# Last two projection units built side by side, convolution LayerNorm several tiles ahead through DRAM, and channel sums by accumulating DMA

## The chip, the cores and the metric

The kernel runs on one core of a Trainium2 chip. The metric is the time of one launch on the device in microseconds (us). The core's engines work in parallel, each in program order: TensorE (PE) multiplies, VectorE (DVE) and ScalarE (ACT) work elementwise, GpSimd (POOL) does small reductions, and SyncE (SP) issues transfers. Transfers that SP issues go by a hardware queue, those that POOL issues by a software queue; sixteen DMA engines carry both. Only transfers from the software queue add to what stands in their destination.

## The reference

One encoder layer on x of 2048 positions by 1024 channels, float32.

```python
h = rms_norm(x, norm_g)
proj = einsum("bsd,de->bse", h, w_in)
a_val, a_gate, g_conv, u, v, g_sgu = split(proj)          # 1024 columns each
c = depthwise_conv(a_val * sigmoid(a_gate), conv_w, conv_b)  # width 31
y_conv = silu(layer_norm(c, conv_ln_g, conv_ln_b)) * silu(g_conv)
y_sgu = u * (mix of layer_norm(v) inside chunks of 128 positions, per head) * silu(g_sgu)
x = x + einsum("bse,ed->bsd", concat(y_conv, y_sgu), w_out)
return rms_norm(x, final_g)
```

## The kernel before

All tiles have 128 partitions. Products take float32 operands split into a high and a low part: `split` lets ScalarE round the value to the high part and VectorE subtract it for the low part, and a product is then three passes of matmuls. The names end in `h` and `l`, or the two halves lie in one tile (`wop`, `op`, `ex`).

The work has four stages. **Group 0 and group 1** project the two halves of the positions. Each has 20 units of 256 output columns; a unit is seven products of half-size blocks in place of eight (`unit_steps`), with 12 matmuls to a product and elementwise sums between them. The operands of each product are built a few products ahead by a list of builders (`build`), seven to a unit, in the units' order. Kinds "c", "s" and "g" are the columns of the convolution, of the spatial gating and of the convolution's gate. After a unit "c" the program emits a convolution (`conv`) of 128 channels at a low priority, so that VectorE does its some 47 multiply-adds where nothing else is ready; the result goes to DRAM as `c_sp`. The tile `cx` in which it is computed comes from a pool of two places.

The **pair phase** multiplies the gating branch by its half of the output weights, two tiles of 128 positions at a time, again with seven products of 12 matmuls for each of eight pairs (`pair_steps`, L742). `pair_operands` loads `ya` and `yb` from DRAM (L718) and splits them into `yh`/`yl`, `qh`/`ql` and `ex`. The seven weight operands `wop` are made once: `wo_raw` loads the four blocks, `wo_put` splits one, `wo_plus` (L709) adds two of them in place. `early(j)` does a part of that during the last unit of group 1. Results leave by SP to `part_sp`.

The **output phase** takes 16 tiles of 128 positions with 48 matmuls each (`out_mm`, L879): the banks `po` are first filled with x plus the pair phase's part (`load_part`: x by SP, then `part_sp` accumulated on it by POOL, into a ring `pring` of four places; `seed_part`, L897, copies it to the banks), then the convolution branch is multiplied by its half of the weights (`woh`, `wol`, split from `hold`). `finish` squares the banks (L904), takes the root, scales into the ring place and stores it to `out`.

The convolution branch of a tile comes from `conv_ln`, a generator of four steps: load the eight channel blocks of 128 positions (`c_ln`, L488) and fold them to a channel sum `csum` (L494 to L496); mean by a matmul with ones, and squares; the inverse deviation; then scaling, the gate's load, silu, the product and the split into `ch` and `cl`, which stay in SBUF. `ln(...)` advances the tiles that it is given by one step each, and `ln_at` lists which steps fall into the pair phase.

A scheduler sets the order of instructions on each engine when the program is built, from these priorities and places; on the chip each engine then keeps to that order, and semaphores guard the data and the reuse of places. Pools are rings: a place comes free when the last reader of its tile is done. The pools that matter here are `wp` (8 places: `w` tiles such as `ch`, `yh`, `op`), `r4` (3 places: `ya`, `yb`, `yq`, `c_ln`), `cx` (2), and in PSUM `ps` (6 banks) and `mx` (2 banks, for the small matmuls).

Of the kernel before, what the change touches and what calls it, by code (L numbers as in the profile page):

```python
# [8 lines left out]
F32 = mybir.dt.float32  # L9
# [5 lines left out]
P = 128  # L15
S = 2048
# [15 lines left out]
def hybrid_block(ctx: ExitStack, tc: tile.TileContext, xt, x, w, wo, wst, vecs, cw, bs, fg, out):  # L32
# [38 lines left out]
    c_sp = dram.tile([NK, P, S], F32, name="c_sp")  # L71
    sgc_sp = dram.tile([NK, P, S], F32, name="sgc_sp")
# [337 lines left out]
    def unit_steps(g, ops, ring, finish):  # L410
# [9 lines left out]
        z = ptile("z")  # L420
# [24 lines left out]
    def conv(i, g):  # L445
# [33 lines left out]
        nc.gpsimd.dma_start(c_sp[i, :, 2 * m0:2 * (m0 + M)], xe.rearrange("p a n -> p (a n)")[:, :2 * M])  # L479
        tc.cur_priority = keep  # L480


    yc = {}

    def conv_ln(ti, c):
# [3 lines left out]
        t = ttile("csum")  # L489
        tt = nc.vector.tensor_tensor  # L490

        def fold(dst, src):
            if dst is not src:
                tt(dst, src[:, 0:512], src[:, 512:1024], op=add)  # L494
            tt(dst[:, 0:256], dst[:, 0:256], dst[:, 256:512], op=add)
            tt(dst[:, 0:P], dst[:, 0:P], dst[:, P:2 * P], op=add)  # L496

        fold(t, c)
# [8 lines left out]
        fold(sq[0], sq[0])  # L507
        yield
        dg = diag_cols(inv_std_cols(partition_sums(sq[0], 1), 1), 1)
        yield  # L510
# [3 lines left out]
        gt = [ttile("gate") for _ in range(2)]  # L514
        for i in range(2):
            nc.sync.dma_start(gt[i].rearrange("p (k s) -> p k s", k=4), sgc_sp[4 * i:4 * i + 4, :, sl].rearrange("k p s -> p k s"))
# [4 lines left out]
        h, l = wtile("ch"), wtile("cl")  # L521
        split(h, l, c)
        yc[ti] = (h, l)
# [56 lines left out]
    def group(g, A, vtiles):  # L580
# [69 lines left out]
        for n, (kind, i) in enumerate(units):  # L650
            steps = unit_steps(g, ops, tiles_of.setdefault(n, []), make[kind](i))
            for j in range(6):
# [21 lines left out]
                if g == 1 and n == NU - 1:  # L674
                    early(j)
# [6 lines left out]
        next(last[0], None)  # L682
        if g == 0:
            return nextA, nv

# [16 lines left out]
    def wo_put(j, q):  # L702
        wo_op[j] = t = btile([P, 2, 4, SG], F32R, f"wop{j}")
        for kp in range(2):
            split(t[:, 0, 2 * kp:2 * kp + 2, :], t[:, 1, 2 * kp:2 * kp + 2, :], raws[kp][q])

    def wo_plus(d, q):
        for kp in range(2):
            nc.vector.tensor_tensor(raws[kp][d], raws[kp][d], raws[kp][q], op=add)  # L709
# [84 lines left out]
    def early(j):  # L794
        if j == 1:
            wo_raw(0)
        if j == 2:
            wo_raw(1)
            wo_put(1, B11)
        if j == 3:  # L800
            prep(0)
            wo_plus(B11, B12)
            wo_put(5, B11)
        if j == 4:
            wo_plus(B11, B22)
            wo_put(6, B11)
            prep(0)
        if j == 5:
            wo_put(2, B21)
# [4 lines left out]
    wo_plus(B12, B22)  # L814
    wo_put(7, B12)
# [5 lines left out]
    lns = {}  # L821

    def ln(*steps):

        for ti in steps:
            if ti >= NT:
                continue
            if ti not in lns:
                c = cx.tile([P, 2, 536], F32, tag="cx", name="c_ln").rearrange("p a n -> p (a n)")[:, :1024] if ti % 4 < 2 else rtile("c_ln")
                lns[ti] = conv_ln(ti, c)  # L830
            next(lns[ti], None)

    ln_at = {(5, 3): (0,), (6, 1): (0,), (6, 3): (1,), (6, 5): (0,), (7, 0): (1, 2), (7, 1): (0,), (7, 2): (1, 3), (7, 3): (2,),
             (7, 4): (1,), (7, 5): (2,)}
    woh, wol, holds = {}, {}, {}
# [13 lines left out]
    for t in range(NT // 2):  # L849
        st = pair_steps(t, pops[t])  # L850
        for j in range(6):
# [8 lines left out]
            if t == NT // 2 - 1:  # L860
                if j == 1:
                    load_wo(0)
                if j == 2:
                    fill_wo(0)
                if j == 4:
                    load_wo(1)
                if j == 5:
                    fill_wo(1)
        last = st
    next(last, None)  # L870
    ln(3, 4)
# [9 lines left out]

    pring = btile([P, 4, 1024], F32, "pring")
    fgt = rtile("fgb")
    nc.sync.dma_start(fgt, fg.partition_broadcast(P))
    parts, pos = {}, {}

    def load_part(ti):
        if ti < NT:
            parts[ti] = pring[:, ti % 4, :]
            nc.sync.dma_start(parts[ti], x[ti * P:(ti + 1) * P, :])  # L890
            nc.gpsimd.dma_start(parts[ti], part_sp[ti], accum_op=add)
# [36 lines left out]
    for ti in range(1, NT):  # L928
        load_part(ti + 3)
# [3 lines left out]
        if ti == NT - 1:  # L933
# [54 lines left out]
```

## Time and profile before

| | before |
|---|---|
| median of 3 runs | 1404.95 us (1404.55 to 1407.33) |
| the profiled execution | 1409.1 us, its span 1407.3 us |
| mean granted TensorE clock | 0.979 of full speed |
| busy in the span: TensorE, VectorE | 1340.2 us (95%), 1190.7 us (85%) |
| busy: ScalarE, GpSimd | 588.4 us (42%), 210.2 us (15%) |
| DMA traffic | 329.15 MB, mean 234 GB/s |

The span runs from the first to the last instruction of the profiled execution. Busy shares are averages over all four stages; the rows below are from the last three of them.

### The profile page before, as it was taken

The numbers are of one execution on the slowest core, as the hardware profiler recorded it, in microseconds if no ns is written. First come the engines' busy times: TensorE is split into PE (matmuls) and PEld (weight loads), VectorE is DVE, ScalarE is ACT, GpSimd is POOL, SyncE is SP. The second block draws the span as 40 slices with busy tenths as digits, with TensorE's granted clock in tenths as the row PEclk, the third lists the DMA queues.
The fourth block names the chain that finished last, engine by engine and source line by source line (L and its number), as shares of the span: only waits on it lengthen the run. The fifth ranks groups of instructions, "written<-read, shape, count | busy, mean of one in ns | idle before, by whom it ended". The sixth has DMA issues, their size and how long they took to land. (4 is left out here: it accounts for less than half of the span.)

```text
span 1407.3 us, 17613 instructions
## 1 busy us (share of the span) xinstructions
PE 1340.2 (95%) x5948; PEld 1099.6 (78%) x5948; DVE 1190.7 (85%) x1865; ACT 588.4 (42%) x985; POOL 210.2 (15%) x394
## 2 busy tenths in 40 slices
PE   7999999999999999999999999999889996998987
PEld 5688888888888778878788888888668885876875
DVE  6985699999999899999899989999999858556753
ACT  5547534444444333443222222222524337545543
POOL 0102322323322301101001101001000001011110
PEclk9999999999999999999999999999989998998999
DMA  6228999989989874389787778787434449667761
GB/s 243 92 79 278 376 330 321 320 297 315 308 292 349 315 250 161 103 271 330 257 263 262 257 255 280 255 281 253 149 97 143 150 122 316 181 180 187 206 167 63
DMA packets 166172, 329.15 MB, mean 234 GB/s; under 512 B 14784, under 2 KB 84416, under 8 KB 166080
## 3 DMA queue, kind: packets, MB, share of 16 engines
q1 hardware_dynamic: 115456, 200.06, 43.9%
q0 software_dynamic: 33728, 119.56, 25.1%
q10 hardware_dynamic: 16896, 8.39, 2.1%
q8 instruction: 47, 0.77, 0.2%
q14 instruction: 45, 0.37, 0.1%
HBM read 191.12 MB, written 136.84 MB: 233 GB/s over the span
## 5 line engine op out<-in xcount | busy, mean ns | idle before, releaser
L469 DVE SCALAR_TENSOR_TENSOR ca<-cx,cwt,ca 128x505 f32<-128x505 f32 (+1 forms) x240 | 180.0, 750 | 0.0
L471 DVE SCALAR_TENSOR_TENSOR cb<-cx,cwt,cb 128x504 f32<-128x504 f32 (+1 forms) x224 | 167.9, 750 | 6.5 <-ACT cb L465 2.8
L477 DVE SCALAR_TENSOR_TENSOR cb<-cq,cws,cb 128x504 f32<-128x504 f32 (+1 forms) x224 | 167.2, 746 | 0.3
L347 PE MATMUL x<-s,op 128*128 128x512 f32 x624 | 153.1, 393 | 1.6 <-ACT s L129 1.4
L347 PEld LDWEIGHTS x<-s,op 128*128 128x128 f32 x624 | 117.7, 189 | 26.7 <-ACT s L129 1.7
L198 PE MATMUL v<-vh,a 128*128 128x512 f32 x448 | 121.0, 393 | 3.8 <-ACT a L129 3.4
L198 PEld LDWEIGHTS v<-vh,a 128*128 128x128 f32 x448 | 84.2, 189 | 23.3 <-ACT a L129 4.2
L347 PE MATMUL z<-s,op 128*128 128x512 f32 x336 | 82.0, 391 | 0.6 <-DVE s L130 0.5
L347 PE MATMUL x<-s,ex 128*128 128x512 f32 x336 | 81.4, 390 | 0.0
L879 PE MATMUL po<-woh,ch 128*128 128x512 f32 x256 | 70.3, 415 | 10.4 <-ACT ch L129 10.4
L347 PE MATMUL x<-a,op 128*128 128x512 f32 x312 | 79.2, 391 | 0.0
L347 PE MATMUL v<-a,op 128*128 128x512 f32 x312 | 75.4, 390 | 2.9 <-DVE t L434 2.9
L347 PE MATMUL y<-a,op 128*128 128x512 f32 x312 | 76.1, 391 | 0.2 <-DMA op<-op_sp 0.2
L347 PE MATMUL v<-s,op 128*128 128x512 f32 x312 | 75.3, 390 | 0.0
L347 PEld LDWEIGHTS z<-s,op 128*128 128x128 f32 x336 | 62.7, 188 | 14.2 <-DVE s L130 0.9
L347 PEld LDWEIGHTS x<-s,ex 128*128 128x128 f32 x336 | 62.9, 188 | 13.0
L130 DVE TENSOR_TENSOR op<-w,op 128x512 fp32r<-128x512 f32 x92 | 62.0, 688 | 10.8 <-ACT op L129 10.8
L347 PEld LDWEIGHTS v<-a,op 128*128 128x128 f32 x312 | 58.3, 188 | 16.3 <-DVE t L434 4.2
L198 PE MATMUL v<-vl,a 128*128 128x512 f32 x224 | 68.5, 394 | 0.9 <-DVE vl L130 0.9
L320 POOL DMA_DIRECT2D op_sp<-op x92 | 49.2, 535 | 133.9 <-DVE op L130 127.9
L129 ACT ACTIVATE op<-w 128x512 fp32r<-128x512 f32 x92 | 54.9, 625 | 33.6 <-DVE w L323 23.5
L347 PEld LDWEIGHTS y<-a,op 128*128 128x128 f32 x312 | 58.4, 188 | 13.1 <-DMA op<-op_sp 0.6
(198 smaller groups left out, 2721.0 us busy)
## 6 DMA issues: line engine op xcount, KB each, us to landing
op_sp<-op POOLq DMA_DIRECT2D x92, 512.0 KB, 6.1
op<-op_sp SPq DMA_DIRECT2D x92, 512.0 KB, 4.8
op_sp<-ex POOLq DMA_DIRECT2D x48, 512.0 KB, 5.8
ex<-op_sp SPq DMA_DIRECT2D x48, 512.0 KB, 5.0
w<-in_w_dram SPq DMA_DIRECT2D x40, 512.0 KB, 7.1
vraw<-in_w_dram SPq DMA_DIRECT2D x32, 256.0 KB, 4.8
mix_sp<-mixt ACTq DMA_DIRECT2D x32, 256.0 KB, 6.4
glu_sp<-sig POOLq DMA_DIRECT2D x64, 128.0 KB, 4.6
```

Of the source, the lines that this page charges most:

```text
L129: nc.scalar.activation(hi, src, AF.Copy)
L130: nc.vector.tensor_tensor(lo, src, hi.bitcast(F32), op=sub)
L198: nc.tensor.matmul(pss[c], A[b, k // 4][:, apart, k % 4, c * P:(c + 1) * P], tiles[k // 2][wpart][:, :, k % 2, :], start=k == 0 and p == 0 ...
L320: nc.gpsimd.dma_start(op_sp[n * 7 + j], t)
L347: nc.tensor.matmul(acc, tv[:, wpart, kk, :], a[:, apart, kk, :], start=start and p == 0 and kk == 0, stop=p == 2 and kk == 3, skip_group_c ...
L469: stt(a, e[:, j:j + M + 1], cwt[:, i, 2 * j:2 * j + 1], a, mul, add)
L471: stt(b, o[:, j:j + M], cwt[:, i, 2 * j + 1:2 * j + 2], b, mul, add)
L477: stt(b, q[:, j:j + M], cws[:, i, j:j + 1], b, mul, add)
L879: nc.tensor.matmul(po[h], lw[:, b * 4 + k, :], rh[:, k, h * SG:(h + 1) * SG], start=False, stop=stop and p == 2 and k == 3, skip_group_che ...
```

## The change

Three things change together, and the places of buffers with them.

The last two units of group 1 (both of kind "s") no longer run one behind the other: their steps alternate, product by product, and their 14 builders alternate too. The bank `z` of both comes from the pool `mx`. `early(j)` runs after each such pair of steps, and the weight operands of the pair phase are split in finer pieces inside it, with those of `wop7` moved in from behind the group.

The convolution's LayerNorm no longer keeps `ch` and `cl` from the LayerNorm to the product: its result is stored to DRAM (`yc_sp`) by POOL, and `load_y` brings it back by SP and splits it two tiles ahead of its use. LayerNorm itself runs three to five tiles ahead; its tiles `c_ln` come from `cx` for the first five and then from a new ring `cring` of four places. The ring `pring` has three places for parts, since its fourth holds the final norm's weights. The gates are loaded one step earlier. The parts and the `yc` of tiles 0 and 1 are loaded during pair 7.

The channel sum is no longer folded by VectorE: each convolution's result is also sent to DRAM `cs_sp`, the first as a store and the other seven of a group as accumulating transfers, and LayerNorm loads 128 columns of it.

```diff
-        nc.gpsimd.dma_start(c_sp[i, :, 2 * m0:2 * (m0 + M)], xe.rearrange("p a n -> p (a n)")[:, :2 * M])
+        flat = xe.rearrange("p a n -> p (a n)")[:, :2 * M]
+        nc.gpsimd.dma_start(c_sp[i, :, 2 * m0:2 * (m0 + M)], flat)
+        if i == 0:
+            nc.gpsimd.dma_start(cs_sp[:, 2 * m0:2 * (m0 + M)], flat)
+        else:
+            nc.gpsimd.dma_start(cs_sp[:, 2 * m0:2 * (m0 + M)], flat, accum_op=add)
         tc.cur_priority = keep
...
     def conv_ln(ti, c):
         sl = slice(ti * P, (ti + 1) * P)
         c3 = c.rearrange("p (k s) -> p k s", k=NK)
         nc.sync.dma_start(c3, c_sp[:, :, sl].rearrange("k p s -> p k s"))
         t = ttile("csum")
+        nc.sync.dma_start(t[:, 0:P], cs_sp[:, sl])
...
-        fold(t, c)
         yield
...
         dg = diag_cols(inv_std_cols(partition_sums(sq[0], 1), 1), 1)
+        gt = [ttile("gate") for _ in range(2)]
+        for i in range(2):
+            nc.sync.dma_start(gt[i].rearrange("p (k s) -> p k s", k=4), sgc_sp[4 * i:4 * i + 4, :, sl].rearrange("k p s -> p k s"))
         yield
...
         for k in range(NK):
             nc.scalar.activation(c3[:, k, :], c3[:, k, :], AF.Silu, bias=cln_b[:, k:k + 1], scale=cln_g[:, k:k + 1])
         for i in range(2):
             tt(c[:, i * SG:(i + 1) * SG], c[:, i * SG:(i + 1) * SG], gt[i], op=mul)
-        h, l = wtile("ch"), wtile("cl")
-        split(h, l, c)
-        yc[ti] = (h, l)
+        nc.gpsimd.dma_start(yc_sp[ti], c)
...
+        if g == 1:
+            tail = builders[-14:]
+            builders[-14:] = [tail[i * 7 + j] for j in range(7) for i in range(2)]
...
-                if g == 1 and n == NU - 1:
-                    early(j)
...
+        both = [unit_steps(g, ops, tiles_of.setdefault(n, []), make[units[n][0]](units[n][1]), xtile) for n in (NU - 2, NU - 1)]
+        for j in range(6):
+            next(both[0])
+            build()
+            if j == 0:
+                next(last[0], None)
+            next(both[1])
+            build()
+            early(j)
+        for steps in both:
+            next(steps, None)
...
     def early(j):
+        if j == 0:
+            wo_raw(0)
         if j == 1:
-            wo_raw(0)
+            wo_put(1, B11, (0,))
         if j == 2:
             wo_raw(1)
-            wo_put(1, B11)
+            wo_plus(B11, B12, (0,))
+            wo_put(5, B11, (0,))
+            wo_put(1, B11, (1,))
         if j == 3:
+            wo_plus(B11, B12, (1,))
+            wo_put(5, B11, (1,))
             prep(0)
-            wo_plus(B11, B12)
-            wo_put(5, B11)
-        if j == 4:
             wo_plus(B11, B22)
             wo_put(6, B11)
+        if j == 4:
             prep(0)
+            wo_put(2, B21)
         if j == 5:
-            wo_put(2, B21)
+            wo_plus(B12, B22)
+            wo_put(7, B12)
     A1, nv = group(0, A, vtiles)
     group(1, A1, nv)
-    wo_plus(B12, B22)
-    wo_put(7, B12)
     wo_put(3, B22)
     wo_plus(B11, B21)
     wo_put(4, B11)
...
@@ -826,13 +844,35 @@
             if ti >= NT:
                 continue
             if ti not in lns:
-                c = cx.tile([P, 2, 536], F32, tag="cx", name="c_ln").rearrange("p a n -> p (a n)")[:, :1024] if ti % 4 < 2 else rtile("c_ln")
+                c = cx.tile([P, 2, 536], F32, tag="cx", name="c_ln").rearrange("p a n -> p (a n)")[:, :1024] if ti < 5 else cring[0][:, ti % 4, :]
                 lns[ti] = conv_ln(ti, c)
             next(lns[ti], None)
-    ln_at = {(5, 3): (0,), (6, 1): (0,), (6, 3): (1,), (6, 5): (0,), (7, 0): (1, 2), (7, 1): (0,), (7, 2): (1, 3), (7, 3): (2,),
-             (7, 4): (1,), (7, 5): (2,)}
-    woh, wol, holds = {}, {}, {}
+    ln_at = {}
+    for i in range(4):
+        for n in (0, 2, 5, 7)[:2 if i == 3 else 4]:
+            ln_at.setdefault(divmod(27 + 5 * i + n, 6), []).append(i)
+    yc = {}
+    def load_y(ti):
+        if ti < NT:
+            r = rtile("yc")
+            nc.sync.dma_start(r, yc_sp[ti])
+            h, l = wtile("ch"), wtile("cl")
+            split(h, l, r)
+            yc[ti] = (h, l)
+    woh, wol = {}, {}
+    parts, pos, pring = {}, {}, []
+    def load_part(ti):
+        if ti < NT:
+            parts[ti] = rtile("part") if ti < 2 else pring[0][:, ti % 3, :]
+            nc.sync.dma_start(parts[ti], x[ti * P:(ti + 1) * P, :])
+            nc.gpsimd.dma_start(parts[ti], part_sp[ti], accum_op=add)
...
             ln(*ln_at.get((t, j), ()))
             if t == NT // 2 - 1:
                 if j == 1:
+                    load_part(0)
+                if j == 2:
                     load_wo(0)
-                if j == 2:
                     fill_wo(0)
+                if j == 3:
+                    load_y(0)
                 if j == 4:
+                    load_part(1)
                     load_wo(1)
+                    load_y(1)
                 if j == 5:
                     fill_wo(1)
         last = st
     next(last, None)
-    ln(3, 4)
+    ln(4)
...
-    for ti in range(3):
-        load_part(ti)
+    pring.append(btile([P, 4, 1024], F32, "pring"))
+    cring.append(btile([P, 4, 1024], F32, "cring"))
+    fgt = pring[0][:, 3, :]
+    nc.sync.dma_start(fgt, fg.partition_broadcast(P))
+    load_part(2)
     seed_part(0)
     seed_part(1)
-    out_mm(pos[0], yc[0], 0, (0, 1), False)
-    ln(2, 3)
-    load_part(3)
-    out_mm(pos[1], yc[1], 0, (0, 1), False)
-    ln(4, 5)
-    out_mm(pos[0], yc[0], 1, (0, 1), True)
-    seed_part(2)
-    finish(0)
-    for ti in range(1, NT):
-        load_part(ti + 3)
+    for ti in range(NT):
+        if ti:
+            load_part(ti + 2)
+        load_y(ti + 2)
         po = pos[ti]
         if ti > 1:
             seed_part(ti + 1)
-        if ti == NT - 1:
+        if ti == 0:
+            out_mm(po, yc[0], 0, (0, 1), False)
+            ln(3, 4)
+            out_mm(pos[1], yc[1], 0, (0, 1), False)
+            out_mm(po, yc[0], 1, (0, 1), True)
+            ln(3, 5)
+            seed_part(2)
+        elif ti < NT - 1:
+            if ti > 1:
+                out_mm(po, yc[ti], 0, (0, 1), False)
+            ln(ti + 3, ti + 4)
+            out_mm(po, yc[ti], 1, (0, 1), True)
+            ln(ti + 3, ti + 5)
+        else:
             for h in range(2):
                 out_mm(po, yc[ti], 0, (h,), False)
                 out_mm(po, yc[ti], 1, (h,), True)
-        else:
-            if ti > 1:
-                out_mm(po, yc[ti], 0, (0, 1), False)
-            ln(ti + 2, ti + 3)
-            out_mm(po, yc[ti], 1, (0, 1), True)
-            ln(ti + 4, ti + 5)
         finish(ti)
```

How the order of instructions moves is shown at three places. The first is VectorE in front of pair 3's first low part, the last row of each excerpt (`ca`, `cb`, `cq` and `cx` are convolutions, `ex` and `ql` operands of pair 2, `oz` and `c` results of a pair). Before:

```order
L777 TENSOR_TENSOR oz_8370<-oz_8370,ox 128x512
L469 SCALAR_TENSOR_TENSOR ca<-cx,cwt,ca 128x521
L477 SCALAR_TENSOR_TENSOR cb<-cq,cws,cb 128x520
L130 TENSOR_TENSOR ex_8213<-ya,ex_8213 128x512
L469 SCALAR_TENSOR_TENSOR ca<-cx,cwt,ca 128x521
L478 SCALAR_TENSOR_TENSOR cx<-cq,cws,cb 128x520
L130 TENSOR_TENSOR ex_8213<-yb,ex_8213 128x1024
L469 SCALAR_TENSOR_TENSOR ca<-cx,cwt,ca 128x521
L130 TENSOR_TENSOR yl<-ya,yh 128x1024
```

The changed kernel:

```order
L744 SCALAR_TENSOR_TENSOR ya<-yq,ya 128x512
L132 TENSOR_TENSOR ql<-yq,qh 128x1024
L473 SCALAR_TENSOR_TENSOR cb<-cx,cwt,cb 128x520
L790 TENSOR_TENSOR oz_8388<-oz_8388,ox 128x512
L132 TENSOR_TENSOR ex_8231<-ya,ex_8231 128x512
L473 SCALAR_TENSOR_TENSOR cb<-cx,cwt,cb 128x520 x4
L132 TENSOR_TENSOR ex_8231<-yb,ex_8231 128x1024
L473 SCALAR_TENSOR_TENSOR cb<-cx,cwt,cb 128x520
L132 TENSOR_TENSOR yl<-ya,yh 128x1024
```

Before, the end of the last convolution but one (`cx<-cq`) stands four rows ahead of `yl`. Now it is fifteen rows ahead, outside the excerpt, and operations of the last convolution take its place. Counted from the start of the program up to this `yl`, there are 9 more convolution operations than before.

The second place is SP, from the load of `ya` for pair 2 or 3 on (`co`, `c` and `oz` are stores of a pair's results). Before, from pair 3's `ya`:

```order
L718 DMA ya<-y_sp 128x8x128
L747 DMA part_sp<-oz_8370 128x512
L747 DMA part_sp<-co 128x512
L718 DMA yb<-y_sp 128x8x128
L488 DMA c_ln<-c_sp 128x8x128
L747 DMA part_sp<-co 128x512
L718 DMA ya<-y_sp 128x8x128
```

The changed kernel, from pair 2's `ya`:

```order
L731 DMA ya<-y_sp 128x8x128
L731 DMA yb<-y_sp 128x8x128
L760 DMA part_sp<-co 128x512
L760 DMA part_sp<-c_8448 128x512
L493 DMA c_ln<-c_sp 128x8x128
L731 DMA ya<-y_sp 128x8x128
L760 DMA part_sp<-oz_8388 128x512
L731 DMA yb<-y_sp 128x8x128
```

The first load of LayerNorm (`c_ln<-c_sp`) stood behind both loads of pair 3; now it stands ahead of them.

The third is TensorE at the end of pair 7 (`ov` and `ox` are its last products, `pc`, `pm` and `rb_c` the small LayerNorm matmuls, `po` the output tiles). Before:

```order
L742 MATMUL ox<-wop_8201,ex_8213 128x512 x12
L512 MATMUL rb_c<-dg,ones 128x128
L742 MATMUL ov<-wop_8208,ex_8213 128x512 x12
L124 MATMUL pc<-ones,csq 128x1
L501 MATMUL pm<-csum,ones 128x128
L512 MATMUL rb_c<-dg,ones 128x128
L124 MATMUL pc<-ones,csq 128x1
L501 MATMUL pm<-csum,ones 128x128
L879 MATMUL po<-woh_9183,ch 128x512 x4
L879 MATMUL po<-woh_9183,cl 128x512 x4
```

The changed kernel:

```order
L126 MATMUL pc<-ones,csq 128x1
L755 MATMUL oy<-wop_8121,yh 128x512 x3
L755 MATMUL ov<-wop_8170,ex_8231 128x512 x4
L755 MATMUL ox<-wop_8219,ex_8231 128x512 x12
L924 MATMUL po<-woh_9285,ch 128x512 x7
L755 MATMUL ov<-wop_8170,ex_8231 128x512 x8
L924 MATMUL po<-woh_9285,ch 128x512
L924 MATMUL po<-woh_9285,cl 128x512 x8
L514 MATMUL rb_c<-dg,ones 128x128
```

The small matmuls of three tiles' LayerNorm stood between the last product and the first output tile. Now one stands between, and the output tile's matmuls begin ahead of the last 8 of pair 7. In each later period of the output phase SP has two loads more, the channel sum and `yc`, and POOL a store to `yc_sp`.

## Rows read from the trace of the kernel before

**Rows 1.** Windows by stage: PE, PEld, DVE, ACT, POOL busy, clock, DMA share, GB/s.

```profile
985.00:1070.40 85.40, 73.75 (x298) 57.06 (x297) 82.58 (x105) 36.52 (x47) 2.69 (x5) 0.92 0.39 130
1070.40:1165.00 94.60, 94.60 (x423) 78.36 (x422) 70.80 (x100) 35.79 (x50) 1.11 (x2) 1.00 0.46 144
1165.00:1191.70 26.70, 14.98 (x61) 11.68 (x59) 24.00 (x37) 20.68 (x40) 4.80 (x7) 0.81 1.01 326
1191.70:1377.00 185.30, 170.82 (x745) 139.03 (x744) 111.82 (x209) 96.15 (x218) 26.93 (x38) 0.94 0.70 183
1377.00:1400.10 23.10, 22.07 (x96) 17.94 (x96) 7.93 (x13) 7.62 (x19) 1.08 (x2) 1.00 0.11 46
```

**Rows 2.** The critical chain at the first product of pair 3.

```profile
1070.44 2.72 PE ox L742 x12
```

**Rows 3.** Waits of TensorE, 985 to 1056: total, times, longest.

```profile
PE ox L742 <- DVE wop L130: 5.2, 1, 5.2
```

**Rows 4.** The critical chain through one round of the part ring.

```profile
1357.22 4.86 DMA out_dram<-pring
1362.10 3.53 DMA pring<-in_x_dram
1365.67 0.46 issue
1366.15 5.42 DMA pring<-part_sp
...
1371.65 1.12 ACT po L897 x2
```

**Rows 5.** Waits in the output phase, 1191.7 to 1400.

```profile
ACT po L897 <- DMA pring<-part_sp: 35.4, 7, 7.4
...
PE po L879 <- ACT ch L129: 10.4, 5, 3.8
```

**Rows 6.** Timeline of VectorE around the end of the fourteenth convolution.

```profile
1060.54 0.76 DVE L469 SCALAR_TENSOR_TENSOR ca<-cx,cwt,ca 128x521 f32<-128x521 f32 x1
1061.21 0.75 DVE L477 SCALAR_TENSOR_TENSOR cb<-cq,cws,cb 128x520 f32<-128x520 f32 x1
...
1063.16 0.75 DVE L478 SCALAR_TENSOR_TENSOR cx<-cq,cws,cb 128x520 f32<-128x520 f32 x1
```

**Rows 7.** Timeline of SP's DMA issues in front of pair 3.

```profile
1060.05 0.37 SPq L718 DMA_DIRECT2D ya<-y_sp  x1
...
1070.24 0.37 SPq L488 DMA_DIRECT2D c_ln<-c_sp  x1
```

**Rows 8.** DMA issues, 1165 to 1191.7: count, size, median us to landing.

```profile
pring<-in_x_dram SPq DMA_DIRECT2D x4, 512.0 KB, 4.9
pring<-part_sp POOLq DMA_DIRECT2D x4, 512.0 KB, 11.8
```

**Rows 9.** DMA queues of the output phase: packets, MB, share of 16 engines.

```profile
q1 hardware_dynamic: 30132, 27.28, 42.5%
q0 software_dynamic: 2101, 7.62, 21.0%
```

**Rows 10.** DMA queues over the whole span, from the page.

```profile
q0 software_dynamic: 33728, 119.56, 25.1%
```

**Rows 11.** Windows around single transfers, and one of the burst (as rows 1).

```profile
1382.00:1385.00 3.00, 3.00 (x15) 2.49 (x14) 1.82 (x2) 1.06 (x1) 0.00 (x0) 1.00 0.43 175
1111.00:1114.50 3.50, 3.50 (x18) 2.88 (x17) 3.36 (x6) 0.19 (x1) 0.00 (x0) 1.00 0.53 150
...
1186.00:1198.00 12.00, 7.70 (x26) 6.04 (x26) 6.28 (x12) 7.61 (x16) 1.42 (x2) 0.62 1.08 240
```

**Rows 12.** Instructions on the tile csum: durations min/median/max in ns.

```profile
L494 DVE TENSOR_TENSOR csum<-c_ln x16: 683/685/693, 1126.2 to 1351.9; 128x512 f32<-128x512 f32 x16
```

**Rows 13.** Timeline of ScalarE: first square of one tile's finish.

```profile
1272.28 0.58 ACT L904 ACTIVATE pring<-po 128x512 f32<-128x512 f32 x1
```

**Rows 14.** Timeline of SP: the output store of that tile.

```profile
1278.37 0.62 SPq L914 DMA_DIRECT2D out_dram<-pring  x1
```

More of the change, by code (lines that the diff above doesn't have):

```diff
@@ L71, in hybrid_block @@
     c_sp = dram.tile([NK, P, S], F32, name="c_sp")
+    cs_sp = dram.tile([P, S], F32, name="cs_sp")
+    yc_sp = dram.tile([NT, P, D], F32, name="yc_sp")
     sgc_sp = dram.tile([NK, P, S], F32, name="sgc_sp")
@@ L408, in finish_g, with unit_steps @@
         return gate, value, False
-    def unit_steps(g, ops, ring, finish):
+    def unit_steps(g, ops, ring, finish, zbank):
         gate, value, odd_first = finish
@@ L419, in unit_steps @@
         yield
-        z = ptile("z")
+        z = zbank("z")
         product(z, s1, ring.pop(0), True)
@@ L478, in conv @@
         stt(res[:, :, 1], q[:, 15:], cws[:, i, 15:16], b, mul, add)
-        nc.gpsimd.dma_start(c_sp[i, :, 2 * m0:2 * (m0 + M)], xe.rearrange("p a n -> p (a n)")[:, :2 * M])
+        flat = xe.rearrange("p a n -> p (a n)")[:, :2 * M]
[4 more added lines that the diff above has]
+            nc.gpsimd.dma_start(cs_sp[:, 2 * m0:2 * (m0 + M)], flat, accum_op=add)
         tc.cur_priority = keep
-    yc = {}
     def conv_ln(ti, c):
@@ L489, in conv_ln @@
         t = ttile("csum")
+        nc.sync.dma_start(t[:, 0:P], cs_sp[:, sl])
         tt = nc.vector.tensor_tensor
[L492 to L496, printed above, removed]
-        fold(t, c)
         yield
@@ L506, in conv_ln @@
         tt(sq[0], sq[0], sq[1], op=add)
-        fold(sq[0], sq[0])
+        tt(sq[0][:, 0:256], sq[0][:, 0:256], sq[0][:, 256:512], op=add)
+        tt(sq[0][:, 0:P], sq[0][:, 0:P], sq[0][:, P:2 * P], op=add)
         yield
         dg = diag_cols(inv_std_cols(partition_sums(sq[0], 1), 1), 1)
+        gt = [ttile("gate") for _ in range(2)]
+        for i in range(2):
+            nc.sync.dma_start(gt[i].rearrange("p (k s) -> p k s", k=4), sgc_sp[4 * i:4 * i + 4, :, sl].rearrange("k p s -> p k s"))
         yield
@@ L513, in conv_ln @@
         tt(c3, c3, rb[:, None, :P].broadcast_to([P, NK, P]), op=mul)
-        gt = [ttile("gate") for _ in range(2)]
-        for i in range(2):
-            nc.sync.dma_start(gt[i].rearrange("p (k s) -> p k s", k=4), sgc_sp[4 * i:4 * i + 4, :, sl].rearrange("k p s -> p k s"))
         for k in range(NK):
@@ L650, in group @@
         for n, (kind, i) in enumerate(units):
-            steps = unit_steps(g, ops, tiles_of.setdefault(n, []), make[kind](i))
+            if g == 1 and n == NU - 2:
+                break
+            steps = unit_steps(g, ops, tiles_of.setdefault(n, []), make[kind](i), ptile)
             for j in range(6):
@@ L681, in group @@
             last = (steps, kind, i)
-        next(last[0], None)
         if g == 0:
+            next(last[0], None)
             return nextA, nv
+        both = [unit_steps(g, ops, tiles_of.setdefault(n, []), make[units[n][0]](units[n][1]), xtile) for n in (NU - 2, NU - 1)]
[3 more added lines that the diff above has]
+            if j == 0:
+                next(last[0], None)
+            next(both[1])
[3 more added lines that the diff above has]
+            next(steps, None)
     wo_op, raws = {}, [[], []]
@@ L700, in wo_raw, with wo_put, wo_plus @@
             raws[kp].append(r)
-    def wo_put(j, q):
-        wo_op[j] = t = btile([P, 2, 4, SG], F32R, f"wop{j}")
-        for kp in range(2):
+    def wo_put(j, q, kps=(0, 1)):
+        if j not in wo_op:
+            wo_op[j] = btile([P, 2, 4, SG], F32R, f"wop{j}")
+        t = wo_op[j]
+        for kp in kps:
             split(t[:, 0, 2 * kp:2 * kp + 2, :], t[:, 1, 2 * kp:2 * kp + 2, :], raws[kp][q])
-    def wo_plus(d, q):
-        for kp in range(2):
+    def wo_plus(d, q, kps=(0, 1)):
+        for kp in kps:
             nc.vector.tensor_tensor(raws[kp][d], raws[kp][d], raws[kp][q], op=add)
@@ L819, in hybrid_block @@
     ex2.append(btile([P, 4, 1024], F32R, "ex2"))
-    lns = {}
+    lns, cring = {}, []
     def ln(*steps):
@@ L880, in out_mm @@
                                      stop=stop and p == 2 and k == 3, skip_group_check=True)
[L882 to L891, printed above, removed]
     def seed_part(ti):
```

## The prediction

> **What bounds the kernel now.** The page gives TensorE the largest busy share, but an average says little, so I read the stages first [rows 1]. At full clock 12 matmuls of a pair take 2.72 us [rows 2], 0.2267 us each; a stage's time less its matmuls at that price is what TensorE loses there.
>
> - 1070.4 to 1165 (pairs 3 to 7): busy throughout at clock 1.00. Nothing is to be won.
> - 985 to 1070.4 (end of the last unit, pairs 0 to 2): 298 matmuls are worth 67.6 us of 85.4, so 17.8 are lost. VectorE is busy 82.58 of 85.4, and TensorE's longest single wait is for VectorE's half of a `wop` split [rows 3]. VectorE is the bound.
> - 1165 to 1191.7 (end of pair 7, start of the output phase): 61 matmuls are worth 13.8 of 26.7, so 12.9 are lost. The DMA share is 1.01: the loads for the output phase come in one burst.
> - 1191.7 to 1400.1: 16 tiles of 48 matmuls are 768 x 0.2267 = 174.1 of 208.4. The 73 small LayerNorm matmuls I put at 6 us (0.08 each, between nothing and 0.2267); about 28 are lost. The chain there [rows 4] runs from an output store through the `x` load into the same ring place, the accumulating load of `part_sp` and its copy into the banks. The waits agree [rows 5]: 35.4 us of ScalarE behind `part_sp`, 10.4 of TensorE behind the split `ch` of LayerNorm's result.
> - From 1400.1 to the span's 1407.3: 7.2 us for the last tile's norm and store.
>
> **Part 1: the last two units and the wop splits.** This stage is VectorE's, so I count VectorE's instructions. The splits move earlier; none is removed. What matters is what the order puts ahead of the pairs' own operands: up to the fourth `yl<-ya` (pair 3) the changed kernel has 9 more convolution operations and nothing less. Such an operation takes 0.75 us alone, but starts stand 0.67 apart [rows 6], so 9 x 0.67 = 6.0 us more work lie in front of pair 3; up to its `ql` it is 6 operations, 4.0 us. I take +5, the middle of the two. Bounds: -17.8, if two units side by side give VectorE enough slack that it is not waited for; +12, if the late `ya` below adds to the 6.
>
> The new wait here is on SP. Pair 3's `ya` was issued at 1060.05, ten microseconds before the first `c_ln` load [rows 7]; now that `c_ln` load stands ahead of it. It takes the `cx` place of the last convolution but one. That one's last operation started at 1063.16 [rows 6]; the new order has it a dozen rows earlier against `yl`, but with more work ahead, so I leave it there. The place now comes free only behind a store to `c_sp` and an accumulation into `cs_sp`. An accumulating load lands in 5.42 [rows 4], so SP gets past it at about 1068; `ya` follows some 4 us later, and pair 3's first product, at 1070.44 before [rows 2], comes at about 1074. Queued behind are the stores of pair 2's results, which nothing waits for before the output phase. It overlaps the 5 us, so I don't add it.
>
> **Part 2: the gap.** `part` and `yc` of tiles 0 and 1 and the `hold` loads are issued inside pair 7, and LayerNorm of tiles 0 to 3 starts earlier. In the new order tile 0's first matmuls stand ahead of pair 7's last 8, and most of the small LayerNorm matmuls that stood between are gone from there. So most of the 12.9 goes: I take -13. Bounds: 0, if these loads still land as late as in the burst (11.8 for a part [rows 8]); -15, with the early matmuls of tile 0.
>
> **Part 3: the output phase.** TensorE's floor is 28 below. Against it stands DMA time, priced as share times time:
> - By queue in this phase [rows 9], over 208.4 us: the hardware queue's 42.5% for 27.28 MB is 3.25 us per MB; the software queue's 21.0% for 7.62 MB is 5.75, so one accumulating part of 0.524 MB costs all sixteen engines 3.0 us. Over the whole kernel, with plain stores for the most part, that queue's 25.1% of 1407.3 is 2.95 per MB [rows 10]: 1.55 for a `yc` store.
> - By short stretches [rows 11]: an `out` store alone is 3.0 x 0.43 = 1.3; a `ya` load alone, in rows of 512 bytes like `c_ln` and the gates, is 3.5 x 0.53 = 1.9.
>
> A period of the changed kernel is out 1.3, x 1.3, part 3.0, gates 1.9, `c_ln` 1.9, `yc` store 1.55 and load 1.3, and a channel sum of 64 KB at 3.25 per MB, 0.2: 12.5 us. TensorE's 48 matmuls are 10.9, with the small ones 11.2. Before, the DMA sum was 9.4. So the DMA engines become the bound as long as LayerNorm runs.
>
> From 1165 on before needs 26.7 x 1.01 + 185.3 x 0.70 + 23.1 x 0.11 = 159 us of DMA [rows 1]. The change adds 14 stores x 1.55, 16 loads x 1.3 and 13 sums x 0.2, 45: 204. About 5 go into pair 7, at a share of 0.46 until 1165; some 43 fall behind tile 9, where LayerNorm is done (three periods of 10.7, one of 7, one of 4). The 156 between, at a share of 1.03 (1.01 and 1.08 where it is saturated [rows 1, 11]), take 151 us from 1170 (1165 + 5): to 1321. TensorE is then about at tile 9's end, 1319; six tiles at 11.2 are 67, the tail 7.2: span 1393. Parts 1 and 2 alone give 1399, so the phase itself yields 6 of its 28.
>
> **A rule against the trace.** In 1186 to 1198 the share was 1.08 at 240 GB/s [rows 11]. The Trainium skill ("DMA: Bandwidth & Descriptors", section "Where 436 GB/s comes from") puts the ceiling at 435 GB/s through 16 ports. By it a period's 3.7 MB would be an estimated 8.6 us, and DMA would not bind. The trace does not agree for this mix, where accumulations cost 5.75 us per MB and rows of 512 bytes half more than whole ones. What the rule would give is the first rival.
>
> **Costed at nothing.** The three folds of the channel sums go (the first takes 0.685 us, 16 times [rows 12]). In the output phase VectorE is busy 111.82 of 185.3, so they save only latency, and LayerNorm now runs three to five tiles ahead. The 16 transfers into `cs_sp`, 0.52 MB or 3.0 us each, stand beside the convolutions, the last ones where the pairs leave the DMA share at 0.39 to 0.46 [rows 1]; each waits for the one before it and holds its `cx` place longer. If a convolution stands still for one: up to +6.
>
> **Sum.** 1407.3 + 5 - 13 - 6 = 1393. The profiled execution took 1409.1 us, the median of the runs is 1404.95; -14 from that is **1391**.
>
> **Rivals.**
> - DMA keeps up and TensorE binds the output phase. For it: the share of 0.70 before. Against it: the prices above. From 1165 the pair's last 13.8 and tile 0's 10.9 lead to 1190; 15 x 11.2 and 7.2 give 1365, with the +5 of part 1 1370: 1363 to 1368 us. Chance 0.14; the skill's rule comes out here.
> - Part 1 gains: side by side, the units fill VectorE's waits and the 17.8 come back in place of +5. 1391 - 23 = 1368. Against it: VectorE is 97% busy there, with more in front. Chance 0.09.
> - No effect: LayerNorm's lead is not what held the phase; the DMA engines reach 0.95 only, as the transfers that wait for one another allow. The 156 take 164 us, the span is 1406, 1404 us. Chance 0.06.
> - Slower: the part ring has three places, not four, so a load can start only a tile later. One round is the finish (6.1 from the first square to the store [rows 13, 14]), out 4.86, x 3.53, issue 0.5, part 5.42, copies 1.1 [rows 4], matmuls 11.2: 32.7 us for three tiles, 10.9 a tile, which leaves no slack at all. In the burst a part takes 11.8, 2.2 times as long, and x 4.9, 1.4 times [rows 8]; with out longer by the one or the other it is 42.4 or 46.2, 14.1 or 15.4 a tile, and at 14.7 the span is 1190 + 15 x 14.7 + 7.2 = 1418, about 1415 us. From 14.2 a tile it is slower than before. Chance 0.18, because a saturated DMA is what I forecast.
>
> The forecast has 0.53, with 1380 to 1402 as its own range. The range for 8 in 10 reaches to the near ends of the fast rivals and of the ring: 1368 to 1413. No change is within 0.2%, 2.8 us, about what runs of this kernel can tell: 1402.1 to 1407.8. Faster: 0.48 of the forecast and both fast rivals, 0.71. Same: no effect and the forecast's upper edge, 0.09. Slower: the ring and the worst of part 1, 0.20.
>
> **What would show it.** Right: pair 3's first product three to five microseconds late with VectorE above 95% ahead of it; no gap before the first `po`; a DMA share of at least 0.95 and 12 to 12.5 us a tile over the first ten tiles, about 11 after. Wrong: 11 us a tile from the start (DMA was no bound); the loss before pair 3 gone (part 1 gains); ScalarE's copies waiting on `part_sp` at 14 us a tile (the ring).

## Result: 3.2% slower, and the profile after

The median is 1451.36 us (4 runs, 1448.82 to 1457.9) against 1406.14 for before (4 runs): ratio 1.0324, 95% interval 1.0283 to 1.0365. It lies outside the forecast range and on its other side. The profiled execution took 1451.84 us with a span of 1450.1.

The windows of the changed kernel (columns as in [rows 1], and three stretches ahead of them):

```profile
0.00:520.00 520.00, 498.18 (x2220) 409.55 (x2220) 446.89 (x731) 248.98 (x404) 127.80 (x242) 0.99 0.82 279
520.00:700.00 180.00, 167.72 (x773) 139.34 (x774) 169.55 (x268) 64.85 (x96) 18.71 (x32) 0.95 0.66 214
700.00:985.00 285.00, 282.42 (x1239) 233.40 (x1238) 264.12 (x389) 71.42 (x104) 35.64 (x73) 0.99 0.81 271
985.00:1076.00 91.00, 80.98 (x334) 64.03 (x333) 86.41 (x110) 36.91 (x49) 6.85 (x13) 0.94 0.50 168
1076.00:1200.80 124.80, 120.34 (x521) 98.36 (x520) 86.78 (x118) 52.31 (x81) 6.03 (x8) 0.97 0.61 181
1200.80:1443.00 242.20, 202.94 (x867) 164.30 (x866) 119.90 (x201) 113.75 (x252) 37.66 (x57) 0.92 0.77 231
```

The last three rows answer to those of [rows 1]: the first to its first, the second to its next two, the third to its last two. Before, up to 985 us:

```profile
0.00:985.00 985.00, 964.00 (x4333) 795.57 (x4334) 891.89 (x1401) 391.09 (x613) 173.02 (x340) 0.99 0.78 264
```

Counting how many matmuls are done by a given time, at 0.2267 us each, places the loss. The changed kernel has done 2220 + 773 + 1239 = 4232 by 985 us, before 4333: **22.9 us are lost in the two groups**, of which the prediction said nothing. By 1040 us only some 9 of them are left, by 1080 it is 21 again, at 1200 it is 13.4: most of the gap ahead of the output phase is gone, as forecast. (The counts take the small LayerNorm matmuls at the same price; with the matmuls of 512 columns alone it is 11.6 at 1200.) Then the output phase, from the first `po` at 1200.83 to the end of the matmuls at 1443, takes 242 us where before needed 208: **the second loss**, 29 us by the counts (13.4 behind at 1200, 42.8 at the end). Its DMA share is 0.77, far from the 1.03 that the sum stood on. Only its first 39 us, up to 1240, are at such a share:

```profile
1200.80:1220.00 19.20, 17.53 (x80) 14.21 (x79) 13.92 (x18) 11.76 (x23) 4.65 (x6) 1.00 1.07 353
1220.00:1240.00 20.00, 11.04 (x49) 8.77 (x47) 4.52 (x8) 6.78 (x16) 1.10 (x2) 0.84 1.07 298
```

From 1240 to 1443 the share is 0.71.

In the groups, TensorE's waits from 470 to 700 us (engine, what it waited for, total, times, longest) are these; the same stretch of before has none above 1.8 us:

```profile
PE z L349 <- ACT s L131: 4.6, 1, 4.6
PE x L349 <- ACT s L131: 4.2, 1, 4.2
PE v L349 <- DVE t L436: 3.0, 1, 3.0
PE v L200 <- ACT vh L131: 2.9, 1, 2.9
```

Waiting is not the whole of the 22.9 us. Up to 985 us TensorE is busy for 948.3 us against 964.0, so 15.7 are idle time; the other 7 are matmuls that took longer, at a lower granted clock. The clearest stretch holds the two longest waits:

```profile
620.00:640.00 20.00, 11.12 (x36) 8.59 (x35) 19.96 (x38) 8.62 (x11) 2.97 (x3) 0.74 0.56 200
```

At full clock the 36 matmuls are 8.2 us; here, with a granted clock of 0.74 on average, TensorE is busy with them for 11.1.

The first wait of the list is for the high part of a block sum `s`, which ScalarE makes when VectorE has its `r`. VectorE's timeline ahead of that `r`, the last row (`ca` and `cb` are operations of a convolution):

```profile
621.86 0.72 DVE L471 SCALAR_TENSOR_TENSOR ca<-cx,cwt,ca 128x505 f32<-128x505 f32 x1
...
622.76 0.69 DVE L479 SCALAR_TENSOR_TENSOR cb<-cq,cws,cb 128x504 f32<-128x504 f32 x1
623.37 0.68 DVE L172 TENSOR_TENSOR r<-a 128x512 f32<-128x512 f32 x1
...
624.09 0.69 DVE L471 SCALAR_TENSOR_TENSOR ca<-cx,cwt,ca 128x505 f32<-128x505 f32 x1
624.70 0.73 DVE L479 SCALAR_TENSOR_TENSOR cb<-cq,cws,cb 128x504 f32<-128x504 f32 x1
625.36 0.68 DVE L173 TENSOR_TENSOR r<-r,r 128x512 f32<-128x512 f32 x1
```

VectorE is not idle; four of these rows are convolution operations, on the path of a waiting TensorE. Before has such rows at this place too, so these rows alone do not explain the wait; the experiments take up what does.

In the output phase the waits that answer to [rows 5] are:

```profile
ACT po L931 <- DMA pring<-part_sp: 40.2, 9, 10.6
...
ACT ch L131 <- DMA yc<-yc_sp: 33.5, 9, 6.7
...
PE po L924 <- ACT ch L131: 25.9, 6, 6.5
...
PE pm L499 <- DMA csum<-cs_sp: 7.3, 2, 6.1
```

`po` waits for `ch` 2.5 times as long as before, and `ch` waits for its load from `yc_sp`. The chain at one such place:

```profile
1264.48 5.24 DMA yc_sp<-c_ln
...
1269.74 5.88 DMA yc<-yc_sp
...
1275.63 0.03 ACT ch L131
```

```profile
1276.74 3.78 PE L924 MATMUL po<-woh,ch 128*128 128x512 f32 x8 [4.41 <-ACT ch L131]
```

LayerNorm's result goes out in 5.2 us and comes back in 5.9, and only then is split; TensorE (the last row, from its timeline) has waited 4.4 us for it. SP shows the second mechanism:

```profile
1210.05 15.51 SPq L493 DMA_DIRECT2D cring<-c_sp  x4
1225.65 3.09 SPq L760 DMA_DIRECT2D part_sp<-c  x1
```

Four LayerNorm loads for the new ring hold SP for 15.5 us, since all four places come with one tile. The stores of pair 7, the first output and the channel sum that TensorE's next `pm` needs stand behind them.

### The profile page after: what moved, and what is told of

It reads as the page before. It is cut to its first block, busy times and chain, and to the rows that moved or that the text cites. A ratio compares the mean times of both kernels' runs of the same rounds, so it can differ in the third digit from the quotient of the medians.

```text
span 1450.1 us, 17718 instructions
## 1 busy us (share of the span) xinstructions
PE 1353.3 (93%) x5948; PEld 1109.3 (76%) x5948; DVE 1175.4 (81%) x1817; ACT 588.9 (41%) x985; POOL 233.2 (16%) x426
## 5 line engine op out<-in xcount | busy, mean ns | idle before, releaser
L924 PE MATMUL po<-woh,ch 128*128 128x512 f32 x256 | 75.8, 436 | 28.9 <-ACT ch L131 25.9
L349 PE MATMUL z<-s,op 128*128 128x512 f32 x348 | 86.2, 395 | 5.9 <-ACT s L131 4.6
L924 PEld LDWEIGHTS po<-woh,ch 128*128 128x128 f32 x256 | 51.8, 210 | 42.5 <-ACT ch L131 28.1
L349 PEld LDWEIGHTS z<-s,op 128*128 128x128 f32 x348 | 65.9, 191 | 20.2 <-ACT s L131 5.1
L349 PE MATMUL y<-a,op 128*128 128x512 f32 x324 | 79.3, 391 | 0.0
L349 PE MATMUL x<-a,op 128*128 128x512 f32 x300 | 76.1, 391 | 0.0
L349 PEld LDWEIGHTS x<-s,ex 128*128 128x128 f32 x348 | 65.1, 188 | 13.4
L420 ACT ACTIVATE y<-x 128x512 f32<-128x512 f32 x40 | 23.3, 581 | 122.1 <-PE x L349 122.1
```

The costliest lines, as they stand in the source:

```text
L349: nc.tensor.matmul(acc, tv[:, wpart, kk, :], a[:, apart, kk, :], start=start and p == 0 and kk == 0, stop=p == 2 and kk == 3, skip_group_c ...
L420: nc.scalar.activation(y, x0, AF.Copy)
L924: nc.tensor.matmul(po[h], lw[:, b * 4 + k, :], rh[:, k, h * SG:(h + 1) * SG], start=False, stop=stop and p == 2 and k == 3, skip_group_che ...
```

## Experiments

Times are medians; ratios are to the runs of before on the same chip, whose median lay between 1407.5 and 1408.4 us. "Ahead" and "behind" are against before, counted in matmuls as above, each from one profiled execution.

### Each part alone

**cs_only**: before, with the third part alone.

```diff
+        if i == 0:
+            nc.gpsimd.dma_start(cs_sp[:, 2 * m0:2 * (m0 + M)], flat)
+        else:
+            nc.gpsimd.dma_start(cs_sp[:, 2 * m0:2 * (m0 + M)], flat, accum_op=add)
...
+        nc.sync.dma_start(t[:, 0:P], cs_sp[:, sl])
...
-        fold(t, c)
```

> Before plus only the third part: the channel sums by accumulating transfers, no folds. Theory (the changed kernel lost 20 to 23 us in the two groups because the transfers into the channel sums hold the convolution's places longer and shift the convolution's operations on VectorE in front of the group's own): it shows that loss alone, 20 to 26 us slower than before, 1425 to 1432 us, with TensorE some 85 to 105 matmuls behind at 900 us. Rival (the group loss comes from another part of the change): within 3 us of before.

Measured 1435.46 us, 1.0195 (1.0163 to 1.0227), 27 us slower, a little more than the theory's 20 to 26, and 26.8 us behind at 980 us. The loss in the groups belongs to the channel sums.

**after_nocs**: the changed kernel without it.

```diff
-            nc.gpsimd.dma_start(cs_sp[:, 2 * m0:2 * (m0 + M)], flat, accum_op=add)
...
-        nc.sync.dma_start(t[:, 0:P], cs_sp[:, sl])
+        tt(t, c[:, 0:512], c[:, 512:1024], op=add)
+        tt(t[:, 0:256], t[:, 0:256], t[:, 256:512], op=add)
+        tt(t[:, 0:P], t[:, 0:P], t[:, P:2 * P], op=add)
```

> The changed kernel with the third part undone (three folds on VectorE, no channel sums in memory). Theory (as for cs_only): the loss in the groups goes, and with it the waits for the sum's load in the output phase: 20 to 30 us faster than the changed kernel, 1421 to 1431 us; what is left above before is the output phase's. Rival: within 3 us of the changed kernel's 1451.

Measured 1422.4 us, 1.0096 (1.0071 to 1.0121): 29 us faster than the changed kernel, as the theory has it, and still slower than before.

**side_only**: before, with the first part alone (`early` with its pieces, too).

```diff
+        both = [unit_steps(g, ops, tiles_of.setdefault(n, []), make[units[n][0]](units[n][1]), xtile) for n in (NU - 2, NU - 1)]
+        for j in range(6):
+            next(both[0])
+            build()
...
+            next(both[1])
+            build()
+            early(j)
```

> Before plus only the first part: last two units side by side, weight operands split earlier. Theory of the prediction (VectorE binds this stretch and has more in front): 0 to 5 us slower than before, 1405 to 1411 us. Rival, suggested by the changed kernel's trace (TensorE regains 14 us from 985 to 1040 and gives part of it back by 1060): 5 to 14 us faster, 1391 to 1400 us.

Measured 1398.24 us, 0.9928 (0.9899 to 0.9956), 10 us faster: the rival, not the prediction. One window of before, then the same of side_only:

```profile
985.00:1060.00 75.00, 63.35 (x252) 48.46 (x251) 72.89 (x92) 31.32 (x40) 2.16 (x4) 0.91 0.35 119
```

```profile
985.00:1060.00 75.00, 70.07 (x306) 56.72 (x304) 73.74 (x94) 34.75 (x45) 2.17 (x4) 1.00 0.41 134
```

Before did 252 matmuls there with VectorE busy 72.89 us. Here VectorE is as busy, and TensorE does 306: 12.2 us gained. Some 7 of them are idle time that is gone (TensorE busy 70.07 us in place of 63.35); the rest is the granted clock, 1.00 in place of 0.91. Its only waits up to 1075 us are four, of 1.9 us at most.

**ln_only**: before, with the second part alone, folds kept.

```diff
-        h, l = wtile("ch"), wtile("cl")
-        split(h, l, c)
-        yc[ti] = (h, l)
+        nc.gpsimd.dma_start(yc_sp[ti], c)
...
+            parts[ti] = rtile("part") if ti < 2 else pring[0][:, ti % 3, :]
```

> Before plus only the second part: LayerNorm ahead through memory, three places for parts, early loads in pair 7, folds kept. Theory (the round trip store, load, split and the burst of four LayerNorm loads on SP cost more than the lead gains): the output phase is 15 to 25 us longer, the gap before it 5 to 10 us shorter, so 5 to 20 us slower than before, 1410 to 1426 us. Rival (the output phase of the changed kernel suffers only from the channel sums' loads): faster than before by 5 to 15 us.

Measured 1423.7 us, 1.0113 (1.0091 to 1.0135). It is 12.2 us ahead at 1200 us, so the gap's gain is real. It is 13.1 behind at 1400 us: the output phase costs 25. The first piece is one wait at its start, in TensorE's row and in SP's:

```profile
1211.74 0.76 PE L495 MATMUL pm<-csum,ones 128*128 128x128 f32 x2 [9.09 <-DVE csum L492]
```

```profile
1187.48 11.74 SPq L487 DMA_DIRECT2D cring<-c_sp  x3
...
1203.14 1.44 SPq L487 DMA_DIRECT2D c_ln<-c_sp  x1
```

Three loads into the ring hold SP for 11.7 us; tile 4's `c_ln`, which `pm` needs, comes behind them.

Alone the parts come to -10, +27 and +15, together 32; the changed kernel is 45 slower. The first two together give +14 (after_nocs), not +5: of the 11.8 us that the units win by 1060, only 2.5 are left at 1200 (14.7 ahead against ln_only's 12.2). What opens the output phase starts no earlier for them.

### What in the channel sums costs it

**cs_plain**: a second plain store, nothing added, folds kept.

```diff
+        nc.gpsimd.dma_start(c2_sp[i, :, 2 * m0:2 * (m0 + M)], xe.rearrange("p a n -> p (a n)")[:, :2 * M])
```

> Before plus a second plain store of each convolution's result to a place of its own in memory; the folds stay, nothing is accumulated. In the groups its order of instructions is that of cs_only, row for row on VectorE. Theory (order and the longer hold of the convolution's place cost the time, not the adding): 15 to 27 us slower than before, 1421 to 1435 us. Rival (the accumulating transfers' own price and their chain): within 5 us of before.

Measured 1430.09 us, 1.0153 (1.0106 to 1.02). At 980 us it is 10.4 behind. Its order on TensorE, ScalarE, VectorE and SP is that of cs_only all through the groups, up to 16 convolution operations ahead of before's on VectorE; so by these counts some 16 of cs_only's 26.8 us come from the adding, and 10.4 from one more transfer with the order that goes with it. The total was as the theory forecast; the split was not. The size of the split is rough: cs_only's profiled execution is the longest of its four, cs_plain's the shortest, and the medians are only 5.4 us apart. That the adding costs time in the groups rests on all four profiles with it (cs_only, cs_dram, best_cs and the changed kernel), which stand 23 to 29 us behind at 985. DMA issues of cs_only over the span, then of cs_plain (its two stores of a result are one row):

```profile
c_sp<-cx POOLq DMA_DIRECT2D x8, 504.0 KB, 4.8
cs_sp<-cx POOLq DMA_DIRECT2D x8, 504.0 KB, 8.2
```

```profile
c_sp<-cx POOLq DMA_DIRECT2D x16, 504.0 KB, 4.9
```

An accumulating transfer takes 3 us longer to land. From 735 to 780 us of cs_only the waits behind it are, on SP's queue and then on the engines:

```profile
SPq L459 <- DMA cs_sp<-cx: 7.4, 1, 7.4
```

```profile
DVE m L388 <- DMA m<-mix_sp: 7.3, 2, 6.7
...
PE v L348 <- DVE t L435: 3.9, 1, 3.9
```

SP waits with the next convolution's load, so what is queued behind it is late; VectorE waits for its `m`, and TensorE, for 3.9 us, for VectorE's `t`. In cs_plain SP's wait there is 3.0 us, and VectorE has none for `m`.

**cs_dram**: the adding transfers read the first copy.

```diff
-            nc.gpsimd.dma_start(cs_sp[:, 2 * m0:2 * (m0 + M)], flat, accum_op=add)
+            nc.gpsimd.dma_start(cs_sp[:, 2 * m0:2 * (m0 + M)], c_sp[i, :, 2 * m0:2 * (m0 + M)], accum_op=add)
```

> As cs_only, but the accumulating transfers read the result from its first copy in memory, so the convolution's place comes free with the first store as in before. Order in the groups as in cs_only. Theory 1 (the order costs the time): 20 to 27 us slower than before. Theory 2 (the longer hold on the chip costs it): within 6 us of before.

Measured 1425.92 us, 1.0119 (1.0077 to 1.0161): 18 us slower, between the two theories, and 28.6 behind at 980 us. Freeing the place early does not help in the groups, so theory 2 falls. Theory 1 isn't shown by it either: the adding is still there and lands in 8.7 to 9.2 us, and from the middle of group 0 its order departs from that of cs_only in places.

**cs_tiny8**: 4 KB in place of 0.5 MB.

```diff
+        nc.gpsimd.dma_start(c2_sp[i, :, 2 * m0:2 * m0 + 8], xe.rearrange("p a n -> p (a n)")[:, :8])
```

> Before plus one more transfer per convolution from its place, of 8 columns only (4 KB), folds kept: no bytes to speak of, but the order on VectorE shifts by up to 7 convolution operations (16 in cs_plain). Theory (the order costs the time): slower than before by 4 to 14 us, 1412 to 1422 us. Rival (bytes on the DMA engines cost it): within 3 us of before.

Measured 1416.56 us, 1.0074 (1.0048 to 1.01). With nearly no bytes, one more transfer and the order that it leads to cost 8 us. Only 1.6 are lost by 980 us and 4.1 by 1200, so this bears the theory out in sign, and only weakly for the groups.

### What in the output phase costs it

**noround5**: after_nocs without the trip through memory from tile 5 on.

```diff
-            r = rtile("yc")
-            nc.sync.dma_start(r, yc_sp[ti])
+            if ti < 5:
+                r = rtile("yc")
+                nc.sync.dma_start(r, yc_sp[ti])
+            else:
+                r = cring[0][:, ti % 4, :]
```

> after_nocs (1422 us) with tiles 5 to 15 split straight from LayerNorm's place in the ring, without the store and load through memory. Theory (the round trip is what makes TensorE wait for the split operand): its waits for that split fall from 23 us to under 10 and the time by 8 to 16 us, 1406 to 1414 us. Rival (the part ring of three places or LayerNorm itself is late): within 4 us of 1422.

Measured 1403.86 us, 0.996 (0.994 to 0.9979), 18.5 faster than after_nocs. TensorE's wait for `ch` from 1200 to 1380 us falls from 18.0 to 6.7:

```profile
ACT ch L130 <- DMA yc<-yc_sp: 10.3, 3, 6.8
...
PE po L924 <- ACT ch L130: 6.7, 4, 2.6
```

The edit takes out the bytes of the round trip together with its landings. That the landings count more is read from the chain above, from after_nocs's DMA share of 0.76 from 1200 to 1380 us, and from 1300 to 1340 us of the changed kernel, where TensorE did 179 matmuls, its full rate, at a share of 0.90; no run takes out one without the other.

**from4**: after_nocs with tile 4's LayerNorm in the ring.

```diff
-                c = cx.tile([P, 2, 536], F32, tag="cx", name="c_ln").rearrange("p a n -> p (a n)")[:, :1024] if ti < 5 else cring[0][:, ti % 4, :]
+                c = cx.tile([P, 2, 536], F32, tag="cx", name="c_ln").rearrange("p a n -> p (a n)")[:, :1024] if ti < 4 else cring[0][:, ti % 4, :]
```

> after_nocs (1422 us) with the LayerNorm input of tile 4 in the new ring too, so that its load goes first and not behind three others that SP issues in a burst. Theory (the 9 to 11 us wait at the start of the output phase comes from that burst): that wait falls under 5 us and the time by 5 to 10 us, 1412 to 1417 us. Rival (the same time is waited for a little later, at the split operand): within 3 us of 1422.

Measured 1414.33 us, 1.0038 (1.0015 to 1.006), 8 faster. The time is the theory's, the mechanism is not: it had the wait fall under 5 us, but the one that ends at 1207 us is still 9.8, now for LayerNorm's squares `csq`, and what is won is won after it.

**noround_ring4**: noround5 with four places for parts.

```diff
-            parts[ti] = rtile("part") if ti < 2 else pring[0][:, ti % 3, :]
+            parts[ti] = rtile("part") if ti < 2 else pring[0][:, ti % 4, :]
...
-    fgt = pring[0][:, 3, :]
+    fgt = rtile("fgb")
```

> noround5 (1404 us) with four places for parts in place of three (the final norm's weights go to another buffer). Theory of the ring rival (three places leave no slack, so ScalarE's copies wait for the part): those waits fall from 34 us to under 15 and the time by 4 to 10 us, 1394 to 1400 us. Rival (the copies' wait is covered, LayerNorm's chain sets the end): within 3 us of 1404.

Measured 1397.93 us (1393.31 to 1402.92), 0.9924 (0.9895 to 0.9954), 6 faster than noround5. ScalarE's wait for the part from 1200 to 1380 us falls from 32.6 to 15.4. The run ranges of the two kernels overlap, so the size is rough.

**noround4_ring4**: the last two together, split straight from tile 4 on.

```diff
-        if ti < 5:
+        if ti < 4:
             nc.gpsimd.dma_start(yc_sp[ti], c)
```

> noround_ring4 with tile 4 too in LayerNorm's ring, split straight from its place. Theory (what is left is the late start of the first LayerNorm tiles, and each trip through memory less helps): 3 to 10 us under noround_ring4, and faster than before and than side_only's 1398. Rival (the wait at the start only moves to the next step of the same chain): within 3 us of noround_ring4.

Measured **1384.58 us**, 0.9841 (0.9819 to 0.9863), 13 under noround_ring4, more than the 3 to 10 expected, and the fastest here. TensorE's rows with a wait in front, the last ones of the span, and the output phase's window:

```profile
1206.47 0.56 PE L125 MATMUL pc<-ones,csq 128*128 128x1 f32 x2 [7.37 <-DVE csq L502]
...
1211.36 0.80 PE L510 MATMUL rb_c<-dg,ones 128*128 128x128 f32 x2 [3.69 <-DVE dg L106]
1213.29 3.78 PE L923 MATMUL po<-woh,ch 128*128 128x512 f32 x8 [1.14 <-ACT ch L130]
```

```profile
1195.00:1377.00 182.00, 168.99 (x763) 139.56 (x761) 116.85 (x218) 102.05 (x228) 25.71 (x38) 0.96 0.68 184
```

From 1214 us on TensorE waits for nothing, at a DMA share of 0.68.

**best_cs**: that kernel with the channel sums again (the edit of cs_only).

> noround4_ring4 (1385 us, the fastest so far) with the channel sums by accumulating transfers put in again. Theory (the accumulating transfers cost some 27 us in the groups, as in cs_only, and little can be won back in an output phase that TensorE already binds): 20 to 30 us slower than noround4_ring4, 1405 to 1415 us. Rival (the loss in cs_only came from its meeting the old last units and output phase): within 8 us of 1385.

Measured 1419.7 us, 1.0085 (1.0059 to 1.0112), 35 slower than noround4_ring4, a little more than forecast. At 1120 us it is 24.7 behind before, where noround4_ring4 is 15.2 ahead.

## Why the prediction was wrong

- **Part 1, +5: wrong in sign.** It took VectorE's 97% for a bound and counted instructions. side_only measures -10 with VectorE just as busy: some 30% of VectorE's work there (32 operations, 24 us) is the convolution, which TensorE does not wait for in that stretch. What held TensorE were single `wop` splits standing late, 5.2 us for the longest [rows 3]; moved earlier, they are not waited for. The rival had the sign; 12.2 us came back of its 17.8.
- **The wait on SP: there, and without effect.** SP stood still between the store at 1077.69 and the `c_ln` load (3.3 us for `cs_sp`), and pair 3's `ya` went out right behind it:

```profile
1077.69 0.33 SPq L760 DMA_DIRECT2D part_sp<-c  x1
1081.36 0.37 SPq L493 DMA_DIRECT2D c_ln<-c_sp  x1
1081.82 0.53 SPq L731 DMA_DIRECT2D ya<-y_sp  x1
```

  Pair 3's first product started at 1091.15 without a wait in front of it. The kernel was 21 us late by then; that this is what hid the wait is argued, not shown.
- **Part 2, -13: right.** 12.2 us in ln_only.
- **Part 3, -6: wrong.** The demand was nearly right: from pair 3 on the windows of the changed kernel give 124.8 x 0.61 + 242.2 x 0.77 + 7.1 x 0.20 = 264 us of DMA, where before had 94.6 x 0.46 + 159 = 203 and the sum added 45. The step that failed is "DMA engines become the bound". Their share was 1.07 only up to 1240 us, and after_nocs loses no less there (TensorE busy 26.8 of the 40 us from 1200) at a share of 0.62. From 1240 to 1443 they were idle for more than a quarter of the time, while LayerNorm's result went out, came back and was split, one transfer behind the other; the burst itself held SP. The sum priced the round trip by its bytes (2.85 us a tile) and not by its latency in the chain (5.2 and 5.9 us). The lead of three to five tiles, which was to hide it, is not there after the burst: the store at 1264.48 is followed at once by the load that TensorE waits for. noround5 shows the cost, 18.5 us. (The sum also goes on from 1319 where its own terms give 1321; these 2 us decide nothing.)
- **"Costed at nothing", 0 to +6: wrong**, the largest miss: +27 alone, +35 in best_cs. It looked for the cost only where the pairs leave the DMA engines free. The transfers stand beside all 16 convolutions, most of them in the groups. They land in 8.0 to 8.2 us, where the prediction took 5.42 from an accumulation into SBUF and plain stores take 4.8 to 5.1; SP's in-order loads wait for the places; and the new order puts up to 16 more convolution operations ahead of the groups' own.
- **The rivals.** The ring was a true mechanism, worth some 6 us in noround_ring4. Its 14.1 to 15.4 us a tile hold the measured 242.2 / 16 = 15.1, but that is luck: most of the time went to the round trip and the burst. "TensorE binds" came about in noround4_ring4, once the round trip was taken out from tile 4 on and the ring had its fourth place again. The ceiling of 435 GB/s from the Trainium skill ("DMA: Bandwidth & Descriptors", section "Where 436 GB/s comes from"), set against the sum as an estimate, had DMA as no bound, and behind 1240 us DMA was none. The trace stays below that ceiling over 5 us: the highest rate of the changed kernel is 420 GB/s, from 275 to 280 us at a share of 1.07.

What stays open: how the 10.4 us of cs_plain divide between the order and the second transfer's bytes, since no run kept before's order with the transfers in it; and why the three parts together cost 13 us more than their sum is argued from the counts at 1200 us, not from a run of its own.

## What to carry to other kernels

An engine that is busy all the time need not be the bound when a part of its work is waited for by nobody: ask which of its instructions somebody waits for, and when they stand in its order. Price a detour through memory by its landings in the chain that it joins, not by its share of the DMA engines, and look at what an in-order queue holds back while one of its loads waits for a place. A sum that is taken off an idle engine and given to a transfer has a cost in every place where that transfer holds a buffer or a queue.

## What was not expected of the hardware

- Accumulating stores of 0.5 MB into memory landed in 8.0 to 8.2 us (median), plain ones of the same tile in 4.8 to 5.1, in the same kernel (cs_only).
- Issuing can block: four LayerNorm loads took SP 15.51 us to issue, one alone 0.37, while the DMA share stood at 1.07.
- A DMA share above 1 went with 420 GB/s in one stretch of the changed kernel (275 to 280 us), with 353 in another (1200.8 to 1220) and with 240 in one of before [rows 11]: bytes per second alone do not say that the engines are full.
